# First loads in one queue, each asked for when a stage of the first tile has passed, and small constants 64 bytes wide

## The chip, the cores and the metric

The kernel runs on one core of a Trainium2 chip. The metric is the device time of one launch in microseconds (us), with all weights and inputs in the chip's memory (HBM) at the start. Everything is float32. One execution was recorded by the hardware profiler, and every duration below comes from that one.

## The reference

A sequence of 512 tokens, 1024 wide, passes two two-layer transformer blocks, one after the other. Each layer is a mixer (several kinds of attention) and a feed-forward part with a short convolution. Only the first steps of the first layer are touched directly:

```python
h = x                                                   # 512 x 1024
y = h * rsqrt(mean(h*h, -1) + EPS) * even_norm1[0]      # rmsnorm
qa, ka, va, qd, kd, vd = split_cols(y @ even_w_in[0], EVEN_IN_SPLIT)
o_a = moba_attention(...);  o_b = diff_attention(...)
h = h + concat(o_a, o_b) @ even_w_out[0]
h = h + conv_ffn(rmsnorm(h, ffn_norm[0]), ...)          # and so on, four layers
```

## The kernel before

**Products.** A float32 product is made of three single-pass products in the type fp32r. Each operand is split into a high part and the rest: activations into hh and hl (or pairs of k tiles), weights into wh and wl. Method mm3 issues the three: low times high (L356), high times low (L357), high times high (L358). In each, one 128-column operand is stationary (loaded into the array first), and the other is streamed past it, mostly 512 columns. In t_tile the weights are stationary ("b<-hh,wl": streamed hh, stationary wl); in r_tile the activations are stationary ("b<-wh,hh", "b<-wh,k", "b<-wh,e"). Transposes and the products of attention weights with values are plain float32 matmuls.

**Weights.** Class Stream loads the weights in the order of use as 455 blocks of at most 512 KB on SyncE's (SP) queue into three buffers wr (RAW = 3). prep makes wh on ScalarE (L299) and wl on VectorE (L300), four buffers each (HB = 4), and then issues the next loads.

**The start.** The tokens lie in four tiles x0 to x3 of 128 tokens. build issues x0, the gain row (512 KB, broadcast to all partitions, on ScalarE's queue), the identity matrix, x1, the first two weight blocks, x2 and x3, all at once. pre_norm returns three stages for a token tile: first, the sum of squares on ScalarE (L420); second, the scale factor on GpSimd (L403, L404) and the scaling on VectorE (L425); third, eight transposes on TensorE (L432) and the split into hh (ScalarE, L390) and hl (VectorE, L391). staged runs the stages of the four tiles as a pipeline, and fill(t) multiplies tile t with the first two weight blocks; vrest multiplies all four tiles with the next two, and so on. The Tile scheduler orders the instructions on each engine when the program is built; at run time each engine takes its own in that fixed order and waits for what it needs.

**Buffers.** All tiles lie in the on-chip memory at fixed places. They are placed one after another in the order of first use, each rounded up to a multiple of 32 bytes per partition. Blocks b8 hands out three tiles of 8192 bytes, named e; the first two are taken by the first pre_norm, the third later. Blocks blk hands out 42 tiles of 2048 bytes, named k. The constants on the way are cols_sb (584 columns, 2336 bytes), mhalf (64 bytes) and neglam (one column, 4 bytes).

Of the kernel before, what the change touches and what calls it, by code (L numbers as in the profile page):

```python
# [9 lines left out]
F32 = mybir.dt.float32  # L10
F32R = mybir.dt.float32r
AF = mybir.ActivationFunctionType
# [4 lines left out]
P, S, D, NT, KT = 128, 512, 1024, 4, 8  # L17
# [234 lines left out]
class Blocks:  # L252


    def __init__(self, pool, prefix, n, shape):
        self.pool, self.shape, self.free, self.tag, self.n = pool, shape, deque(f"{prefix}{i}" for i in range(n)), {}, 0
        self.prefix = prefix
# [15 lines left out]
class Stream:  # L273


    def __init__(self, k, w, plan):
        self.k, self.w, self.plan = k, w, plan
        self.loaded = self.prepped = self.lo = self.hi = 0
        self.raw, self.parts = {}, {}

    def load(self):
        i = self.loaded
        raw = self.k.sb.tile([P, CH], F32, name=f"wr{i}", tag="wr", bufs=RAW)
        n = self.plan[i][2]
        self.k.nc.sync.dma_start(raw[:, :n], self.w[i, :, :n])
        self.raw[i] = raw
        self.loaded += 1
# [36 lines left out]
class Kernel:  # L324
# [63 lines left out]
    def split(self, hi, lo, src):  # L388

        self.nc.scalar.copy(hi, src)  # L390
        self.nc.vector.tensor_sub(lo, src, hi.bitcast(F32))  # L391
# [16 lines left out]
    def pre_norm(self, gsrc, goff, queue=None):  # L408

        nc = self.nc  # L410
        e = self.b8.get()
        grow = e[:, :D]
        (queue or nc.sync).dma_start(grow, self.row(gsrc, goff, D))
        hb = self.b8.get()
        hs = [hb[:, :D], hb[:, D:]]
        ss = {}

        def sumsq(t):
            s = self.small()
            nc.scalar.activation(e[:, D:], self.x[t], AF.Square, accum_out=s)  # L420
            ss[t] = s

        def scale(t):
            r = self.rstd(ss.pop(t), 1.0 / D)
            nc.vector.scalar_tensor_tensor(hs[t % 2], self.x[t], r, grow, op0=ALU.mult, op1=ALU.mult)  # L425

        def turn(t):
            for half in range(2):
                b = self.bank(2 * t + half)
                for j in range(4):  # L430
                    c = (4 * half + j) * P
                    nc.tensor.transpose(b[:, j * P:(j + 1) * P], hs[t % 2][:, c:c + P], self.ident)  # L432
                src = b.rearrange("p (k q) -> p k q", k=4)
                dst = (slice(None), slice(4 * half, 4 * half + 4), slice(t * P, (t + 1) * P))
                self.split(self.hh[dst], self.hl[dst], src)

        def end():
            self.b8.put(e, hb)

        def first(t):  # L440
            sumsq(t)

        def second(t):
            scale(t)

        self.junk = e[:, D:]
        return [first, second, turn], end
# [147 lines left out]
class Job:  # L595
# [15 lines left out]
    def tail(self):  # L611
        return self._tail(self)
# [127 lines left out]
class Block1:  # L740
# [69 lines left out]
        return tail  # L810

    def start(self):
        self.first = self.k.pre_norm(self.k.a["even_norm1"], 0, self.k.nc.scalar)

    def even(self):
        k, nc, a = self.k, self.k.nc, self.k.a
        stages, end = self.first
        Va, Vd = {}, {}
        parts, vb = [], {}

        def fill(t):
            if not parts:
                parts.extend(k.ws.get(*[("e", "va", c) for c in range(2)]))
            vb[t] = k.bank(2 * t)
            for c in range(2):
                k.r_tile(vb[t], parts[c], t, (2 * c, 2 * c + 1), S, start=c == 0, stop=c == 3)

        k.staged(stages, fill)
        end()
        self.vrest("e", "va", 2, vb, Va)  # L830
        vb = {t: k.bank(2 * t + 1) for t in range(NT)}
        self.vrest("e", "vd", 0, vb, Vd)
        self.lam()
        self.tables()
        nc.sync.dma_start(k.cols, a["cols"])
        at, n = COLS[2, "bg"]
        nc.vector.tensor_scalar(k.cols[:, at:at + 2 * n], k.cols[:, at:at + 2 * n], 0.5, None, op0=ALU.mult)
        store, out, tabs = {}, {}, {}

        def begin(p):  # L840
            def f(job):
                if p < 4:
                    tabs[p] = [self.table(2 * p), self.table(2 * p + 1)]
                else:
                    tabs[p] = [self.table(4 + p)] * 2
            return f

        def free_qk(p, tail):
            def f(job):
                fns = tail(job)  # L850
                first = fns[0]

                def g():
                    k.blk.put(*store.pop(p))
                    k.blk.put(tabs[p][0])
                    if p < 4:
                        k.blk.put(tabs[p][1])
                    first()
                    if p == 3:
                        k.blk.put(*Va.values())  # L860
                return [g] + fns[1:]
            return f

        def tab(p):
            return lambda hd, t, n: tabs[p][hd][:, 384 - t * P:]

        jobs = []
        for p in range(4):
            jobs.append(Job(k, Job.PAIR, self.heads64(store, p), tab(p), out, lambda p=p: p in store, begin(p),
                            free_qk(p, self.pair_tail(Va, lambda hd, p=p: (2 * p + hd) * 64, store, p, tabs, out, p))))  # L870
        for h in range(4):
            p = 4 + h
            jobs.append(DiffJob(k, self.heads64(store, p), tab(p), out, lambda p=p: p in store, begin(p),
                                free_qk(p, self.diff_tail(Vd, h, out, p))))

        def dense():
            for p in range(8):
                while p - 2 in store:
                    yield NEED
                yield from self.qk_proj("e", p, store)  # L880
            while 3 not in out:
                yield NEED
            yield from self.out_half("e", out)

        k.weave(dense(), k.attention(jobs), 800)
        k.blk.put(*Vd.values())
        return self.out_rest("e", out, 0)
# [9 lines left out]
            V[t] = k.blk.get()  # L897
            k.evac(V[t], vb[t])

    def lam(self):  # L900
        k, nc, a = self.k, self.k.nc, self.k.a
        b = k.blk.get()
        nc.sync.dma_start(b[:, :256], k.row(a["diff_lambda"], 0, 256))
        v = b[:, :256].rearrange("p (a b d) -> p a b d", a=2, b=2)
        pr = b[:, 256:384].rearrange("p (a d) -> p a d", a=2)
        s, e = k.small(2), k.small(2)
        nc.vector.tensor_mul(pr, v[:, :, 0], v[:, :, 1])
        nc.vector.tensor_reduce(s, pr, axis=mybir.AxisListType.X, op=ALU.add)
        nc.scalar.activation(e, s, AF.Exp)
        nc.vector.tensor_sub(k.neglam, e[:, 1:2], e[:, 0:1])  # L910
        nc.vector.tensor_scalar_add(k.neglam, k.neglam, -0.2)
        nc.sync.dma_start(k.subln, k.row(a["diff_subln"], 0, P))
        nc.vector.tensor_scalar(k.subln, k.subln, 0.8, None, op0=ALU.mult)
        k.blk.put(b)
# [926 lines left out]
def build(tc, a, plan):  # L1841
    nc = tc.nc
    with ExitStack() as ctx:
        sb = ctx.enter_context(tc.tile_pool(name="sb", bufs=1))
        ps = ctx.enter_context(tc.tile_pool(name="ps", bufs=1, space=PSUM))
        dram = ctx.enter_context(tc.tile_pool(name="dram", bufs=1, space=DRAM))
        k = Kernel(tc, a, plan, sb, ps, dram)
        k.x = [k.const(f"x{t}", [P, D]) for t in range(NT)]
        xin = a["x"][0].rearrange("(t p) d -> t p d", p=P)
        k.ident = k.const("ident_sb", [P, P])  # L1850
        k.cols = k.const("cols_sb", [P, a["cols"].shape[1]])
        b1 = Block1(k)
        nc.sync.dma_start(k.x[0], xin[0])
        b1.start()
        nc.scalar.dma_start(k.ident, a["ident"])
        nc.sync.dma_start(k.x[1], xin[1])
        k.ws.load()
        k.ws.load()
        for t in range(2, NT):
            nc.sync.dma_start(k.x[t], xin[t])  # L1860
        k.mhalf = k.const("mhalf", [P, 16])
        nc.gpsimd.memset(k.mhalf, -0.5)
        k.neglam = k.const("neglam", [P, 1])
        k.subln = k.const("subln_sb", [P, P])
        k.hh = k.const("hh", [P, KT, S], F32R)
        k.hl = k.const("hl", [P, KT, S], F32R)
        ff = b1.even()
        ff = b1.odd(ff)
        b2 = Block2(k)
        ff = b2.mix(0, ff)  # L1870
        ff = b2.mix(1, ff)
        b2.end(ff)
# [39 lines left out]
```

## Time and profile before

| | us |
|---|---|
| median of three runs | 2867.37 (2866.7 to 2872.15) |
| the profiled execution | 2869.32 |
| its span on the core | 2867.5 |
| TensorE busy | 2822.6 |
| TensorE's first instruction | 14.63 |
| first matmul with weights | 19.35 |

The profile gives for each engine its busy time, for groups of instructions the line, the operation, out<-in by the program's names (buffer numbers left out) and the mean duration, and in the timeline each instruction with its start. Engines are PE (TensorE matmul), PEld (its loads of the stationary operand), DVE (VectorE), ACT (ScalarE), POOL (GpSimd) and SP (SyncE); a q behind the name is the engine's queue. TensorE's granted clock is 0.999 of full speed over the span. The duration of a matmul contains the pipeline's depth, so in a stream the distance from one start to the next is what each costs.

### The profile page before, as it was taken

Reading aid. Unit: us, or ns where it says so; the run is one execution under the profiler, and the core shown is the slowest. Engines: PE = TensorE matmul, PEld = TensorE weight load, DVE = VectorE, ACT = ScalarE, POOL = GpSimd, SP = SyncE. Lnnn points to the kernel's source line nnn. Section 1 sums busy time; section 2 is a strip of 40 time slices with the busy share of each in tenths; the row PEclk is TensorE's granted clock in tenths of the full one; section 3 lists DMA queues with packets and bytes.
Section 4 is the critical chain, followed back from the end, with each engine's and each line's share of the span. In section 5 each row is a group of like instructions: output and inputs, shape, how many; then the busy total and the mean of one; then the engine's idle time right before and its main releaser. Section 6 shows DMA issues by size and latency. Waiting matters only on the chain.

```text
span 2867.5 us, 34913 instructions
## 1 busy us (share of the span) xinstructions
PE 2822.6 (98%) x13612; PEld 2309.6 (81%) x13612; DVE 1538.3 (54%) x2687; ACT 1112.3 (39%) x1928; POOL 102.8 (4%) x192
## 2 busy tenths in 40 slices
PE   7999999999999999999999999999999999999999
PEld 6778888888788888787777888888887777888887
DVE  4566544244764443377655465552685544666633
ACT  3453433224533332245433344441454434344421
POOL 1000000000000000020000010000120000100000
PEclk9999999999999999999999999999999999999999
DMA  4542323334322233232234222333221332333232
GB/s 160 156 127 83 103 96 101 104 100 129 100 85 95 95 101 103 79 99 79 79 100 123 97 96 95 103 103 101 89 86 63 103 118 89 103 96 99 95 101 74
DMA packets 93651, 287.19 MB, mean 100 GB/s; under 512 B 12544, under 2 KB 15488, under 8 KB 93486
## 3 DMA queue, kind: packets, MB, share of 16 engines
q1 hardware_dynamic: 92526, 283.18, 31.6%
q8 instruction: 107, 1.75, 0.3%
q10 hardware_dynamic: 864, 1.64, 0.2%
q14 instruction: 58, 0.48, 0.1%
q0 software_dynamic: 96, 0.14, 0.0%
HBM read 258.38 MB, written 2.15 MB: 91 GB/s over the span
## 4 chain that ended last, share of the span: by engine, by line
PE 68%; issue 24%; DVE 4%; DMA 2%; POOL 1%; ACT 1%; SPq 0%; POOLq 0%; DVEq 0%; ACTq 0%
PE b L356 21%; PE b L358 21%; PE b L357 21%; PE b L1528 1%; PE b L655 1%; DMA k<-k 1%; PE b L362 1%; POOL s L404 1%; DMA wr<-in_w_dram 1%; DVE wl L300 1%; PE b L1783 1%; PE b L432 1%; PE b L1831 0%; DVE e L425 0%; PE b L1812 0%
## 5 line engine op out<-in xcount | busy, mean ns | idle before, releaser
L356 PE MATMUL b<-hh,wl 128*128 128x512 f32 (+1 forms) x2368 | 903.6, 382 | 1.6 <-ACT hh L390 1.0
L358 PE MATMUL b<-hh,wh 128*128 128x512 f32 (+1 forms) x2368 | 898.1, 379 | 0.0
L357 PE MATMUL b<-hl,wh 128*128 128x512 f32 (+1 forms) x2368 | 897.3, 379 | 0.0
L300 DVE TENSOR_TENSOR wl<-wr,wh 128x1024 fp32r<-128x1024 f32 (+1 forms) x421 | 511.5, 1217 | 538.8 <-ACT wh L299 536.8
L299 ACT CAST wh<-wr 128x1024 fp32r<-128x1024 f32 (+1 forms) x421 | 438.0, 1042 | 474.5 <-PE b L358 429.8
L356 PEld LDWEIGHTS b<-hh,wl 128*128 128x128 f32 x2368 | 445.1, 188 | 89.8 <-issue 7.9
L358 PEld LDWEIGHTS b<-hh,wh 128*128 128x128 f32 x2368 | 445.8, 188 | 83.4 <-issue 1.4
L357 PEld LDWEIGHTS b<-hl,wh 128*128 128x128 f32 x2368 | 446.2, 188 | 80.2 <-issue 2.0
L356 PE MATMUL b<-wh,k 128*128 128x512 f32 x900 | 352.9, 392 | 0.0
L357 PE MATMUL b<-wl,k 128*128 128x512 f32 x900 | 351.0, 390 | 0.0
L358 PE MATMUL b<-wh,k 128*128 128x512 f32 x900 | 350.6, 390 | 0.0
L356 PEld LDWEIGHTS b<-wh,k 128*128 128x128 f32 x900 | 169.1, 188 | 35.7 <-issue 0.8
L358 PEld LDWEIGHTS b<-wh,k 128*128 128x128 f32 x900 | 169.0, 188 | 35.4
L357 PEld LDWEIGHTS b<-wl,k 128*128 128x128 f32 x900 | 169.0, 188 | 33.9
L1231 ACT ACTIVATE e<-b,cols_sb 128x512 f32<-128x512 f32 x88 | 68.3, 776 | 153.7 <-PE b L358 153.7
L1232 DVE SCALAR_TENSOR_TENSOR e<-b,cols_sb,e 128x511 f32<-128x511 f32 x88 | 65.7, 746 | 104.6 <-ACT e L1231 104.4
L1221 DVE SCALAR_TENSOR_TENSOR e<-b,cols_sb,e 128x511 f32<-128x511 f32 x44 | 33.0, 749 | 159.2 <-ACT e L1220 159.2
L1220 ACT ACTIVATE e<-b,cols_sb 128x512 f32<-128x512 f32 x44 | 34.3, 778 | 178.1 <-PE b L358 178.1
L632 ACT ACTIVATE k<-k,s 128x256 f32<-128x256 f32 (+4 forms) x144 | 75.2, 523 | 59.5 <-DVE s L630 55.7
L357 PE MATMUL b<-wl,hh 128*128 128x512 f32 (+2 forms) x256 | 92.8, 362 | 0.4 <-DVE wl L300 0.4
L356 PE MATMUL b<-wh,hl 128*128 128x512 f32 (+2 forms) x256 | 93.1, 364 | 0.0
L358 PE MATMUL b<-wh,hh 128*128 128x512 f32 (+2 forms) x256 | 91.8, 360 | 0.0
(192 smaller groups left out, 3021.7 us busy)
## 6 DMA issues: line engine op xcount, KB each, us to landing
wr<-in_w_dram SPq DMA_DIRECT2D x451, 512.0 KB, 3.5
k<-k SPq DMA_DIRECT2D x186, 128.0 KB, 2.4
k<-brev SPq DMA_DIRECT2D x20, 256.0 KB, 4.0
x<-in_x_dram SPq DMA_DIRECT2D x4, 512.0 KB, 7.4
k<-in_rpb_dram SPq DMA_DIRECT2D x16, 128.0 KB, 3.2
wr<-in_w_dram SPq DMA_DIRECT2D x4, 448.0 KB, 3.2
e<-in_ffn_norm_dram SPq DMA_DIRECT2D x2, 512.0 KB, 3.7
e<-in_norm_mix_pre_dram SPq DMA_DIRECT2D x2, 512.0 KB, 4.5
```

The lines of the kernel that those rows point to most:

```text
L299: nc.scalar.copy(hi[:, :n], raw[:, :n])
L300: nc.vector.tensor_sub(lo[:, :n], raw[:, :n], hi[:, :n].bitcast(F32))
L356: mm(out, sl, mh, start=start, stop=False)
L357: mm(out, sh, ml, start=False, stop=False)
L358: mm(out, sh, mh, start=False, stop=stop)
L362: self.nc.tensor.matmul(out, s, m, start=i == 0, stop=i == len(pairs) - 1)
L404: nc.gpsimd.tensor_tensor(r, a, self.mhalf[:, :w], op=ALU.pow)
L632: nc.scalar.activation(s[:, c], s[:, c], AF.Exp, bias=mx[:, i:i + 1], scale=-1.0, accum_out=sm[:, i:i + 1])
L1220: nc.scalar.activation(c, b, AF.Identity, bias=self.col(("cb",), m), scale=self.col(("cw", 2), m))
L1221: nc.vector.scalar_tensor_tensor(c[:, 1:], b[:, :S - 1], self.col(("cw", 1), m), c[:, 1:], op0=ALU.mult, op1=ALU.add)
L1231: nc.scalar.activation(y, b, AF.Identity, bias=self.col(("cb",), mm), scale=self.col(("cw", 1), mm))
L1232: nc.vector.scalar_tensor_tensor(y[:, 1:], b[:, :S - 1], self.col(("cw", 0), mm), y[:, 1:], op0=ALU.mult, op1=ALU.add)
```

## The change

x0 and the gain row go first on SP's queue, in that order. The other first loads are held back: before each stands a one-column copy on GpSimd into the buffer that is to be loaded, which reads a column of a result that has to be there first. The two first weight blocks wait for x0's sum of squares (through a new constant, passed), x1 for x0's scaling, x2 for x0's second split, x3 for x1's first split, and the next weight blocks for x0's second split. The vectors for lam, subln and cols wait for the last tile's split. The identity goes first on ScalarE's queue, and a small Square on mhalf stands ahead of the first sum of squares. neglam grows from one column to 16, mhalf moves ahead of the e tiles, and passed (16 columns) is new.

```diff
 class Stream:
     def __init__(self, k, w, plan):
+        self.passed = None
     def load(self):
         raw = self.k.sb.tile([P, CH], F32, name=f"wr{i}", tag="wr", bufs=RAW)
+        if self.passed is not None:
+            self.k.nc.gpsimd.tensor_copy(raw[:, :1], self.passed)
         self.k.nc.sync.dma_start(raw[:, :n], self.w[i, :, :n])
...
-        hs = [hb[:, :D], hb[:, D:]]
+        hs = self.normed = [hb[:, :D], hb[:, D:]]
...
     def start(self):
-        self.first = self.k.pre_norm(self.k.a["even_norm1"], 0, self.k.nc.scalar)
+        self.first = self.k.pre_norm(self.k.a["even_norm1"], 0)
...
-        stages, end = self.first
+        (first, second, turn), end = self.first
+        passed = k.const("passed", [P, 16])[:, :1]
+        def ask(t, stage):
+            nc.gpsimd.tensor_copy(k.x[t][:, :1], stage)
+            nc.sync.dma_start(k.x[t], xin[t])
...
-        k.staged(stages, fill)
+        def sumsq(t):
+            first(t)
+            if t == 0:
+                nc.gpsimd.tensor_copy(passed, k.junk[:, :1])
+                k.ws.passed = passed
+                k.ws.load()
+                k.ws.load()
+        def scale(t):
+            second(t)
+            if t == 0:
+                ask(1, k.normed[0][:, :1])
+        def split(j, t):
+            return k.hl[:, j, t * P:t * P + 1].bitcast(F32)
+        def last(t):
+            turn(t)
+            if t < 2:
+                ask(2 + t, split(4 - 4 * t, t))
+            k.ws.passed = split(4, 0) if t == 0 else None
+            fill(t)
+        k.staged([sumsq, scale, last])
...
-        self.lam()
+        self.lam(split(4, NT - 1))
         self.tables()
+        nc.gpsimd.tensor_copy(k.cols[:, :1], split(4, NT - 1))
         nc.sync.dma_start(k.cols, a["cols"])
...
+        k.mhalf = k.const("mhalf", [P, 16])
+        nc.gpsimd.memset(k.mhalf, -0.5)
+        nc.scalar.dma_start(k.ident, a["ident"])
+        nc.scalar.activation(k.small(16), k.mhalf, AF.Square)
         nc.sync.dma_start(k.x[0], xin[0])
         b1.start()
-        nc.scalar.dma_start(k.ident, a["ident"])
-        nc.sync.dma_start(k.x[1], xin[1])
-        k.ws.load()
-        k.ws.load()
-        for t in range(2, NT):
-            nc.sync.dma_start(k.x[t], xin[t])
-        k.mhalf = k.const("mhalf", [P, 16])
-        nc.gpsimd.memset(k.mhalf, -0.5)
-        k.neglam = k.const("neglam", [P, 1])
+        k.neglam = k.const("neglam", [P, 16])[:, :1]
```

The order on the engines moves at the start alone. VectorE up to the first tiles' splits, before (numbers tell instances apart; wr_75 and wr_77 are the first two weight blocks, x_63 to x_66 the token tiles):

```order
L300 TENSOR_TENSOR wl_139<-wr_75,wh_138 128x1024
L300 TENSOR_TENSOR wl_147<-wr_77,wh_146 128x1024
L425 SCALAR_TENSOR_TENSOR e_72<-x_63,s_90,e_70 128x1024
L425 SCALAR_TENSOR_TENSOR e_72<-x_64,s_111,e_70 128x1024
L425 SCALAR_TENSOR_TENSOR e_72<-x_65,s_132,e_70 128x1024
L391 TENSOR_TENSOR hl<-b_5_96,hh 128x4x128
L391 TENSOR_TENSOR hl<-b_6_103,hh 128x4x128
```

and now (line numbers are four higher):

```order
L429 SCALAR_TENSOR_TENSOR e_77<-x_63,s_93,e_75 128x1024
L395 TENSOR_TENSOR hl<-b_6_101,hh 128x4x128
L304 TENSOR_TENSOR wl_118<-wr_86,wh_117 128x1024
L395 TENSOR_TENSOR hl<-b_7_108,hh 128x4x128
L304 TENSOR_TENSOR wl_128<-wr_89,wh_127 128x1024
L429 SCALAR_TENSOR_TENSOR e_77<-x_64,s_162,e_75 128x1024
L429 SCALAR_TENSOR_TENSOR e_77<-x_65,s_198,e_75 128x1024
L395 TENSOR_TENSOR hl<-b_12_168,hh 128x4x128
```

The first tile's scaling and splits now stand ahead of, and between, the two weight blocks.

GpSimd after its three table loads, before:

```order
L403 TENSOR_SCALAR s_89<-s_87 128x1
L404 TENSOR_TENSOR s_90<-s_89,mhalf 128x1
L403 TENSOR_SCALAR s_110<-s_94 128x1
L404 TENSOR_TENSOR s_111<-s_110,mhalf 128x1
L403 TENSOR_SCALAR s_131<-s_115 128x1
L404 TENSOR_TENSOR s_132<-s_131,mhalf 128x1
```

and now:

```order
L407 TENSOR_SCALAR s_92<-s_83 128x1
L288 COPY wr_86<-passed 128x1
L288 COPY wr_89<-passed 128x1
L408 TENSOR_TENSOR s_93<-s_92,mhalf 128x1
L828 COPY x_64<-e_77 128x1
L828 COPY x_65<-hl 128x1
L288 COPY wr_121<-hl 128x1
L288 COPY wr_124<-hl 128x1
L288 COPY wr_131<-hl 128x1
L407 TENSOR_SCALAR s_161<-s_99 128x1
L408 TENSOR_TENSOR s_162<-s_161,mhalf 128x1
```

The copies that hold loads back stand between the scale factors; the second tile's factor (s_162) stands behind five of them.

The places of the buffers move for the whole program. Start in each partition in bytes, by the two built programs, with the remainder to 64 in brackets:

| tile | before | after |
|---|---|---|
| first and second e | 35744, 43936 (32) | 38368, 46560 (32) |
| three wr, from | 52128 (32) | 88160 (32) |
| hh, hl | 65024, 81408 (0) | 55328, 71712 (32) |
| four wh, from | 100352 (0) | 100448 (32) |
| four wl, from | 116736 (0) | 116832 (32) |
| 42 k, from | 133120 (0) | 133216 (32) |
| third e | 151552 (0) | 151648 (32) |

Before, cols_sb (2336 bytes) leaves the remainder 32, and neglam, rounded from 4 to 32 bytes, takes it away again for all that lies behind. After, mhalf, neglam and passed take 64 bytes each.

## Rows read from the trace of the kernel before

**Rows 1.** The page, busy time, share of the span and instructions of each engine.
```profile
PE 2822.6 (98%) x13612; PEld 2309.6 (81%) x13612; DVE 1538.3 (54%) x2687; ACT 1112.3 (39%) x1928; POOL 102.8 (4%) x192
```
**Rows 2.** Timelines of the start: start us, us, engine line op out<-in [idle before].
```profile
6.05 1.06 ACT L420 ACTIVATE e<-x 128x1024 f32<-128x1024 f32 x1 [3.10 <-DMA x<-in_x_dram]
7.29 0.18 POOL L403 TENSOR_SCALAR s<-s 128x1 f32<-128x1 f32 x1 [4.23 <-ACT e L420]
7.56 0.57 POOL L404 TENSOR_TENSOR s<-s,mhalf 128x1 f32<-128x1 f32 x1
...
10.88 2.50 DVE L300 TENSOR_TENSOR wl<-wr,wh 128x1024 fp32r<-128x1024 f32 x2 [10.88 <-ACT wh L299]
...
13.29 1.28 DVE L425 SCALAR_TENSOR_TENSOR e<-x,s,e 128x1024 f32<-128x1024 f32 x1
...
14.63 5.07 PE L432 MATMUL b<-ident_sb,e 128*128 128x128 f32 x21 [14.63 <-DVE e L425]
...
19.35 0.78 PE L356 MATMUL b<-wh,hl 128*128 128x512 f32 x1
...
43.18 0.59 ACT L398 COPY k<-b 128x512 f32<-128x512 f32 x1 [2.13 <-PE b L358]
```
**Rows 3.** The page, DMA issues: out<-in, xcount, size each, median us to landing.
```profile
wr<-in_w_dram SPq DMA_DIRECT2D x451, 512.0 KB, 3.5
...
x<-in_x_dram SPq DMA_DIRECT2D x4, 512.0 KB, 7.4
```
**Rows 4.** Matmuls by line, tiles and shape: count | busy us, mean ns.
```profile
L356 PE MATMUL b<-hh,wl 128*128 128x512 f32 x2112 | 832.4, 394 | 0.6 <-DVE k L1606 0.6
...
L356 PE MATMUL b<-wh,k 128*128 128x512 f32 x900 | 352.9, 392 | 0.0
...
L356 PE MATMUL b<-k,wl 128*128 128x512 f32 x220 | 87.9, 399 | 1.2 <-DVE k L1606 0.7 <-DVE k L391 0.5
...
L356 PE MATMUL b<-hh,wl 128*128 128x256 f32 x256 | 71.2, 286 | 1.0 <-ACT hh L390 1.0
L356 PE MATMUL b<-wh,hl 128*128 128x512 f32 x160 | 63.2, 396 | 0.0
...
L356 PE MATMUL b<-wh,hl 128*128 128x256 f32 x64 | 18.1, 283 | 0.0
```
**Rows 5.** Tile e, 610 to 650 us (first layer): duration ns min/median/max.
```profile
L432 PE MATMUL b<-ident_sb,e x32: 270/272/329, 623.6 to 643.7; 128*128 128x128 f32 x32
L356 PE MATMUL b<-wh,e x16: 394/394/400, 613.8 to 634.4; 128*128 128x512 f32 x16
L357 PE MATMUL b<-wl,e x16: 392/399/399, 614.1 to 634.6; 128*128 128x512 f32 x16
L358 PE MATMUL b<-wh,e x16: 390/392/394, 614.3 to 634.9; 128*128 128x512 f32 x16
```
**Rows 6.** The same, 1195 to 1235 us (second layer).
```profile
L356 PE MATMUL b<-wh,e x16: 389/389/395, 1196.8 to 1219.5; 128*128 128x512 f32 x16
L357 PE MATMUL b<-wl,e x16: 389/389/393, 1197.0 to 1219.8; 128*128 128x512 f32 x16
L358 PE MATMUL b<-wh,e x16: 389/389/389, 1197.2 to 1220.0; 128*128 128x512 f32 x16
```
**Rows 7.** Timeline of PE, first and last of twelve in a row, first layer.
```profile
619.39 0.39 PE L356 MATMUL b<-wh,e 128*128 128x512 f32 x1
...
621.96 0.39 PE L358 MATMUL b<-wh,e 128*128 128x512 f32 x1
```
**Rows 8.** The same, second layer.
```profile
1202.22 0.39 PE L356 MATMUL b<-wh,e 128*128 128x512 f32 x1
...
1204.71 0.39 PE L358 MATMUL b<-wh,e 128*128 128x512 f32 x1
```
**Rows 9.** The same, 838 to 872 us (transposes between the first two layers).
```profile
L432 PE MATMUL b<-ident_sb,e x32: 270/272/276, 841.6 to 866.1; 128*128 128x128 f32 x32
```
**Rows 10.** Tile e streamed in plain float32 (L1528), the whole span.
```profile
L1528 PE MATMUL b<-e,k x128: 592/592/645, 1339.8 to 2260.4; 128*64 128x512 f32 x128
```

More of the change, by code (lines that the diff above doesn't have):

```diff
@@ L812, in start @@
     def start(self):
-        self.first = self.k.pre_norm(self.k.a["even_norm1"], 0, self.k.nc.scalar)
+        self.first = self.k.pre_norm(self.k.a["even_norm1"], 0)
     def even(self):
         k, nc, a = self.k, self.k.nc, self.k.a
-        stages, end = self.first
+        (first, second, turn), end = self.first
         Va, Vd = {}, {}
         parts, vb = [], {}
+        xin = a["x"][0].rearrange("(t p) d -> t p d", p=P)
+        passed = k.const("passed", [P, 16])[:, :1]
+        def ask(t, stage):
+            nc.gpsimd.tensor_copy(k.x[t][:, :1], stage)
+            nc.sync.dma_start(k.x[t], xin[t])
         def fill(t):
@@ L898, in vrest, with lam @@
             k.evac(V[t], vb[t])
-    def lam(self):
+    def lam(self, passed):
         k, nc, a = self.k, self.k.nc, self.k.a
         b = k.blk.get()
+        nc.gpsimd.tensor_copy(b[:, :1], passed)
+        nc.gpsimd.tensor_copy(k.subln[:, :1], passed)
         nc.sync.dma_start(b[:, :256], k.row(a["diff_lambda"], 0, 256))
```

## The prediction

> **What bounds the kernel now.** I read the busy times first. TensorE is busy for 2822.6 of 2867.5 us, 98%; VectorE has 54% and ScalarE 39% [rows 1]. So two things can move the time: the 45 us in which TensorE is idle, and the duration of its matmuls. Of the idle time 14.6 us lie at the start in one piece [rows 2], and 30 us are spread over the rest. The change means to move the first piece. But it also moves every buffer, so after the timeline of the start I looked at matmuls whose operands lie at different places.
>
> At the start, x0's sum of squares begins at 6.05 us and its scale factor is ready at 8.13 (7.56 + 0.57), yet the scaling comes at 13.29, since VectorE's order has both weight blocks first (10.88 and 2.50 long). So transposes start at 14.63 and weight matmuls at 19.35, and from there TensorE runs on: the first bank of the first product is copied out until 43.18 [rows 2], and its 96 matmuls of 0.226 [rows 8] and the late transposes fill that stretch. What the change can win is that this end at 43.2 comes sooner.
>
> **The start, step by step.** A 512 KB block lands a median of 3.5 us after its issue in the stream, and the four x tiles, all asked at once, took 7.4 [rows 3]. Now x0 goes nearly alone: I take 4.5 us as its landing (ends: 3.5 after the issue, or 6.05 as now). Sum of squares 1.25, then GpSimd: its order is the copy into passed, the first half of the factor, two copies into wr, the second half. Copies aren't in the trace; the small operation at 7.29 has 0.18 and the next starts 0.27 later [rows 2], so four steps of 0.27 and 0.57 end at about 7.4. VectorE scales until 8.7 (1.28), eight transposes, about a microsecond (21 took 5.07 with their waits [rows 2]), end at 9.7. The weights, asked at 6.5, land at 10.0 and 11.2; their splits (1.06 on ScalarE, as an operation of that width took, 1.25 on VectorE [rows 2]), mixed with x0's splits, let the first matmuls start at 12.5 instead of 19.35.
>
> That is 7 us sooner, but it isn't kept. After x0's 12 matmuls TensorE waits for x1, whose load was asked at 9.0, and now the tiles follow each other by landings: copy 0.3, landing 3.5, sum 1.25, factor 0.85, scaling 1.28, transposes 1, split 1.3 make 9.5 us for one tile. x2 is asked when x0's second split is done (13.2), x3 when x1's first split is done, and VectorE's order puts x2's scaling ahead of that split, so x3 is asked at about 21.3 and lands at 25. Its split ends at 30.4. Of the 96 matmuls 52 are then left, 11.8 us, which end at 42.5. The gain at 43.2 is 0.7 us. Ends: with 2.5 us for a landing and no stall the work itself, 25 us from 12.5, ends at 37.4, 6 us won; with the slow rows (7.4 for a landing once, copies that wait behind a VectorE operation of 1.28) 4 us are lost. Queued behind the waiting copies on GpSimd are the factors of x1 to x3, which the order shows, and they are in this walk. The vectors for lam and cols are asked some 15 us later than now and used from the first attention on; their cover is the 96 matmuls of the next product, 22 us. The extra Square on ScalarE runs before x0 has landed. Both at nothing.
>
> **The places of the buffers.** Before, hh, hl, wh, wl, the k tiles and the third e start at a multiple of 64 bytes; the first two e and wr lie 32 bytes off. After, all of them lie 32 off: 2336 bytes of cols_sb leave 32, and neglam, 32 bytes before, no longer takes it away. Whether that costs can be read from the trace of before, since an e tile is now and then the stationary operand of a single-pass matmul. In the first layer that tile is one that lies 32 off: medians of 394, 399 and 392 ns for the three lines [rows 5]. In the second layer the same lines, the same shapes, work on the third e, which starts at a multiple of 64: 389, 389 and 389 [rows 6]. Mean difference 6.0 ns. Starts say the same: twelve in a row take 2.57 us for 11 distances in the first layer [rows 7], 233.6 ns each, and 2.49 in the second [rows 8], 226.4; difference 7.3, with 0.01 us of rounding at each end. I take 6.7. The streamed operand is a wh or wl, at 0 in both, so it is the stationary one that pays.
>
> Plain float32 shows nothing of it: transposes of an e that lies 32 off have a median of 272 ns [rows 5], of the third e 272 too [rows 9]. And streamed e tiles of both kinds take 592 ns at the minimum and the median alike [rows 10]. So only single-pass matmuls pay, by their stationary operand.
>
> After the change nearly all of them do. In [rows 4] stand the groups of L356, and L357 and L358 have as many: (2112 + 900 + 220 + 256 + 160 + 64) x 3 = 11,136 matmuls, and their stationary operands are wl, wh, hl, hh and k, all moved from 0 to 32. At 6.7 ns that is 74.6 us (66.8 at 6.0, 81.3 at 7.3). TensorE is busy without a gap through them, so it lies on the path. I take 3 us off for the 30 us of spread idle time, where a wait may shrink because TensorE comes later; the attention's score matmuls, which I haven't counted, may add as much. For VectorE and ScalarE no row here splits by place; they have 46% and 61% of idle time as cover [rows 1]. DMAs into wr land 32 off already.
>
> The streamed operand moves too. No row shows a streamed fp32r operand that lies 32 off; the nearest is plain float32, with no cost [rows 10], and from above I bound it by what the stationary one pays, another 75 us. I take 0, as the row says.
>
> **Sum.** -0.7 + 74.6 - 3 = +71 us. Against the profiled execution (2869.32, 2867.5 of span) that is 2940; the median of the runs is 2 us lower, so 2938. Own range of this case: 6.0 ns and the best start give +58, 7.3 ns, no absorption and the worst start +88, so 2925 to 2955.
>
> **Rivals.**
> First, not slower: the place as such costs nothing. Then the difference in [rows 5, 6] comes from the two operands lying differently (32 against 0), and as both move by 32 it is gone. Its price is 0 instead of 74.6, and it decides as soon as the matmuls keep their distance of 226 ns. Time: the start alone, 2867.4 - 0.7 = 2867, with the start's ends 2861 to 2871. For it: I have seen no pair with both operands at 32. Against it: the slower pace stays through twelve matmuls [rows 7], whichever of wh and wl is streamed.
> The Trainium skill, page "SBUF — State Buffer", section "Specifications (TRN2)", gives lines of 16 bytes for the memory. A tile that lies 32 off starts on such a line as well as one at 64; by that rule the new places cost nothing, the same 2867. The trace doesn't agree: 394, 399 and 392 ns against 389 [rows 5, 6].
>
> Second: the streamed operand pays as well, another 74.6 us: 2938 + 75 = 3013. For it: the streamed 2048 bytes come from the same memory, and fp32r streams in one pass, 226 ns from start to start, where plain float32 takes longer and may hide it. Against it: [rows 10].
>
> Third, that the change does what it says and wins: x0's 7 us are kept. It needs landings of 2.5 us for x1 to x3, and gives 6 us at the most, less than a tenth of what the places cost; it is in the ranges above.
>
> **Chances.** Stationary operand pays: 0.70. Both pay: 0.10. Neither pays: 0.20. A measurement of this kernel can tell about 0.2%, 5.7 us, from no change. The first two are slower. Of the third, 0.14 lies within 0.2%, 0.05 is faster by more, 0.01 slower. So slower 0.81, same 0.14, faster 0.05. The range takes in the first and the third case, 2860 to 2960, and leaves out the second and the tails.
>
> **What would show it.** In the profile after: the groups of L360 to L362 with a mean 6 to 7 ns above [rows 4] and the medians of the second layer's e matmuls at 394, 399, 392 as in [rows 5]; TensorE's busy time near 2897. If they stay at 389, the first rival holds; at 13 ns more, the second. At the start: the first weight matmul near 12.5, a pause of some 5 us before x1's, the end of the first product at 42 to 43. I am wrong if the matmuls keep their pace, or if the start alone moves the end by more than 6 us.

## The result, and the profile after

The changed kernel takes 2901.55 us, the median of four runs (2899.24 to 2903.69), against 2867.86 for the kernel before on the same chip. The ratio is 1.0117, with a 95% interval from 1.0105 to 1.0129: slower by about 33.7 us. The forecast was 2938, with a range of 2925 to 2955 for its main case. The sign is right, and the place too (TensorE's matmuls take longer), but the size is a little under half of the 71 us that were said.

The page of the kernel after, busy time, share of the span (2901.9 us) and instructions, which answers to [rows 1]:

```profile
PE 2856.9 (98%) x13612; PEld 2307.0 (79%) x13612; DVE 1538.9 (53%) x2687; ACT 1113.8 (38%) x1929; POOL 105.1 (4%) x206
```

TensorE is busy 34.3 us longer with the same 13,612 matmuls, and idle for 45.0 us as before (44.9). The span grew by 34.4. So the whole difference is longer matmuls, and no new wait. Which ones, the groups of TensorE tell, by line, tiles and shape (xcount | busy us, mean ns | idle before), which answer to [rows 4]:

```profile
L360 PE MATMUL b<-hh,wl 128*128 128x512 f32 x2112 | 843.8, 400 | 0.6 <-DVE k L1642 0.6
L362 PE MATMUL b<-hh,wh 128*128 128x512 f32 x2112 | 837.9, 397 | 0.0
L361 PE MATMUL b<-hl,wh 128*128 128x512 f32 x2112 | 836.9, 396 | 0.0
L360 PE MATMUL b<-wh,k 128*128 128x512 f32 x900 | 352.7, 392 | 0.0
...
L360 PE MATMUL b<-k,wl 128*128 128x512 f32 x220 | 87.8, 399 | 1.2 <-DVE k L1642 0.7 <-DVE k L395 0.5
...
L360 PE MATMUL b<-hh,wl 128*128 128x256 f32 x256 | 70.2, 282 | 1.0 <-ACT hh L394 1.0
L360 PE MATMUL b<-wh,hl 128*128 128x512 f32 x160 | 64.3, 403 | 0.8 <-ACT wh L303 0.8
```

Two groups of the kernel before that were not shown yet, for the other two lines of mm3:

```profile
L358 PE MATMUL b<-hh,wh 128*128 128x512 f32 x2112 | 826.2, 391 | 0.0
L357 PE MATMUL b<-hl,wh 128*128 128x512 f32 x2112 | 824.9, 391 | 0.0
```

Three things are to be seen. The groups that stream hh or hl past wh or wl with 512 columns grew by 11.4, 11.7 and 12.0 us: 35.1 us, which is the whole result. The groups with k as an operand, 3360 matmuls on three lines, did not move: 352.9 to 352.7, 87.9 to 87.8, although k moved by as many bytes as wh. And the same hh with 256 columns became faster, 71.2 to 70.2 on this line. A cost that every moved stationary operand pays would have raised all three.

The start, from the timeline of all engines (start us, us, engine line op out<-in, idle before), which answers to [rows 2]:

```profile
4.99 1.06 ACT L424 ACTIVATE e<-x 128x1024 f32<-128x1024 f32 x1 [2.29 <-DMA x<-in_x_dram]
...
7.59 1.28 DVE L429 SCALAR_TENSOR_TENSOR e<-x,s,e 128x1024 f32<-128x1024 f32 x1 [7.59 <-POOL s L408]
8.93 1.57 PEld L436 LDWEIGHTS b<-ident_sb,e 128*128 128x128 f32 x8 [8.93 <-DVE e L429]
8.93 1.97 PE L436 MATMUL b<-ident_sb,e 128*128 128x128 f32 x8 [8.93 <-DVE e L429]
8.94 0.18 POOL L828 COPY x<-e 128x1 f32<-128x1 f32 x1 [1.38 <-DVE e L429]
...
11.69 0.79 PE L360 MATMUL b<-wh,hl 128*128 128x512 f32 x1 [0.79 <-ACT wh L303]
...
13.56 1.11 POOL L828 COPY x<-hl 128x1 f32<-128x1 f32 x1 [4.43 <-DVE hl L395]
13.71 1.06 ACT L424 ACTIVATE e<-x 128x1024 f32<-128x1024 f32 x1 [0.64 <-DMA x<-in_x_dram]
13.97 0.63 PE L360 MATMUL b<-wh,hl 128*128 128x512 f32 x1
...
14.40 0.63 PE L361 MATMUL b<-wl,hh 128*128 128x512 f32 x1
...
15.98 1.28 DVE L429 SCALAR_TENSOR_TENSOR e<-x,s,e 128x1024 f32<-128x1024 f32 x1 [1.35 <-POOL s L408]
...
16.85 0.40 PE L361 MATMUL b<-wl,hh 128*128 128x512 f32 x1
16.85 0.19 PEld L362 LDWEIGHTS b<-wh,hh 128*128 128x128 f32 x1
17.08 0.40 PE L362 MATMUL b<-wh,hh 128*128 128x512 f32 x1
17.32 0.86 PEld L436 LDWEIGHTS b<-ident_sb,e 128*128 128x128 f32 x8 [0.28 <-DVE e L429]
...
21.79 0.87 PE L436 MATMUL b<-ident_sb,e 128*128 128x128 f32 x6 [3.37 <-DVE e L429]
...
23.53 0.33 SPq L829 DMA_DIRECT2D x<-in_x_dram  x1
```

and the last copy of the first product, on ScalarE (its start stands for the end of that product, here and in the runs below):

```profile
44.92 0.59 ACT L402 COPY k<-b 128x512 f32<-128x512 f32 x1 [2.16 <-PE b L362]
```

x0's scaling comes at 7.59 instead of 13.29, and the first weight matmul at 11.69 instead of 19.35, more than 7 us sooner. But TensorE then waits for tiles (3.37 us ahead of x2's transposes alone), the last tile is asked for only at 23.53, and the first product ends at 44.92, 1.7 us later than the 43.18 of [rows 2].

### The profile page after: what moved, and what is told of

Its sections match the earlier page's. It is cut to its first block, busy times and chain, and to the rows that moved or that the text cites. A ratio compares the mean times of both kernels' runs of the same rounds, so it can differ in the third digit from the quotient of the medians.

```text
span 2901.9 us, 34939 instructions
## 1 busy us (share of the span) xinstructions
PE 2856.9 (98%) x13612; PEld 2307.0 (79%) x13612; DVE 1538.9 (53%) x2687; ACT 1113.8 (38%) x1929; POOL 105.1 (4%) x206
## 3 DMA queue, kind: packets, MB, share of 16 engines
q10 hardware_dynamic: 720, 1.11, 0.1%
## 4 chain that ended last, share of the span: by engine, by line
PE 68%; issue 25%; DVE 3%; DMA 2%; POOL 1%; ACT 1%; SPq 0%; POOLq 0%; DVEq 0%; ACTq 0%
PE b L360 21%; PE b L362 21%; PE b L361 21%; PE b L659 1%; PE b L1564 1%; DMA k<-k 1%; POOL s L408 1%; PE b L366 1%; PE b L1819 1%; PE b L1867 0%; PE b L1849 0%; DVE wl L304 0%; PE b L1848 0%; DVE e L429 0%; DMA x<-in_x_dram 0%
## 5 line engine op out<-in xcount | busy, mean ns | idle before, releaser
L360 PE MATMUL b<-hh,wl 128*128 128x512 f32 (+1 forms) x2368 | 914.0, 387 | 1.6 <-ACT hh L394 1.0
L362 PE MATMUL b<-hh,wh 128*128 128x512 f32 (+1 forms) x2368 | 908.6, 384 | 0.0
L361 PE MATMUL b<-hl,wh 128*128 128x512 f32 (+1 forms) x2368 | 908.0, 384 | 0.0
L360 PE MATMUL b<-wh,k 128*128 128x512 f32 x900 | 352.7, 392 | 0.0
L1256 ACT ACTIVATE e<-b,cols_sb 128x512 f32<-128x512 f32 x44 | 34.3, 779 | 184.3 <-PE b L362 184.3
L400 DVE COPY e<-b 128x512 f32<-128x512 f32 (+1 forms) x112 | 63.1, 564 | 55.7 <-PE b L1867 24.8
```

The lines of the kernel that those rows point to most:

```text
L360: mm(out, sl, mh, start=start, stop=False)
L361: mm(out, sh, ml, start=False, stop=False)
L362: mm(out, sh, mh, start=False, stop=stop)
L400: self.nc.vector.tensor_copy(out, src)
L1256: nc.scalar.activation(c, b, AF.Identity, bias=self.col(("cb",), m), scale=self.col(("cw", 2), m))
```

## The experiments

**The question.** Two theories fit what the kernel before showed in [rows 5, 6]. Theory A, the prediction's: a single-pass matmul pays when its stationary operand starts 32 bytes off a multiple of 64, wherever the streamed one lies. Theory B: it pays when its two operands start at different places modulo some power of two, wherever they lie. The table of places in the section on the change gives remainders to 64, by which hh and wh look alike after the change. To 256 they don't:

| tile | before, mod 256 | after, mod 256 |
|---|---|---|
| first and second e | 160 | 224 |
| hh, hl | 0 | 32 |
| wh, wl, k, third e | 0 | 96 |

So by theory B hh and hl have gone apart from wh and wl by 64, k has stayed with wh and wl, and the e tiles were the pair that lay apart before. The kernels below move single buffers, by constants that nobody reads, and leave all work as it is unless it is said.

**b_pad64: the kernel before, with the weights and k moved by 64 bytes.** All stationary operands stay at multiples of 64; hh and hl part from wh and wl by 64.

```diff
         k.hl = k.const("hl", [P, KT, S], F32R)
+        pad = k.const("padw", [P, 16])
+        k.nc.gpsimd.memset(pad, 0.0)
```

> The kernel before, its order untouched, with a 64-byte constant placed between hl and wh: hh and hl keep the remainder 0 to 256 bytes, and wh, wl, the k tiles and the third e move to the remainder 64. All starts that were multiples of 64 still are. Own place (the theory of the prediction: a stationary operand that lies 32 bytes off a multiple of 64 pays): no change, 2867 us, the groups of hh with wl and wh stay at 379 to 394 ns. Distance (what counts is the distance between the starts of the stationary and the streamed operand, modulo 256): the 6336 matmuls of 512 columns with hh streamed past wh or wl go from 227 to 233 ns from start to start, as in the changed kernel, +35 us, 2902 us; the groups wh with k keep 390 to 392.

Measured: 2896.82 us, ratio 1.0098 (1.0082 to 1.0115). TensorE's groups:

```profile
L356 PE MATMUL b<-hh,wl 128*128 128x512 f32 x2112 | 843.0, 399 | 0.6 <-DVE k L1606 0.6
L358 PE MATMUL b<-hh,wh 128*128 128x512 f32 x2112 | 837.1, 396 | 0.0
L357 PE MATMUL b<-hl,wh 128*128 128x512 f32 x2112 | 835.9, 396 | 0.0
L356 PE MATMUL b<-wh,k 128*128 128x512 f32 x900 | 352.7, 392 | 0.0
...
L356 PE MATMUL b<-hh,wl 128*128 128x256 f32 x256 | 70.0, 281 | 1.0 <-ACT hh L390 1.0
```

The same three groups grow as after the change (10.6, 10.9 and 11.0 us), k stays, and 256 columns gain. Nothing of the start was touched and no operand left its multiple of 64. Theory A falls: it gives no change here. A 64-byte constant in the wrong place costs this kernel 28.6 us.

**a_near: the change, with passed placed ahead of hh.** In the order of the places passed then stands before the big tiles, so hh, hl, wh, wl, k and the third e all start at 96 modulo 256. All of them still lie 32 off a multiple of 64.

```diff
+        k.passed = k.const("passed", [P, 16])[:, :1]
         k.subln = k.const("subln_sb", [P, P])
...
-        passed = k.const("passed", [P, 16])[:, :1]
+        passed = k.passed
```

> The changed kernel with passed placed ahead of subln instead of behind hl, so that hh, hl, wr, wh, wl, k and the third e all have the remainder 96 to 256; order and waits stay. Own place: all still lie 32 off a multiple of 64, no change against the changed kernel, 2901 us. Distance: all of hh, wh, wl and k lie alike, the 6336 matmuls go back to 227 ns, -35 us; what stays is the start, 1 to 2 us later than in the kernel before: 2868 to 2870 us.

Measured: 2869.67 us, ratio 1.0006 (0.9996 to 1.0015).

```profile
L360 PE MATMUL b<-hh,wl 128*128 128x512 f32 x2112 | 832.0, 394 | 0.6 <-DVE k L1642 0.6
L362 PE MATMUL b<-hh,wh 128*128 128x512 f32 x2112 | 826.0, 391 | 0.0
L361 PE MATMUL b<-hl,wh 128*128 128x512 f32 x2112 | 824.3, 390 | 0.0
```

The means are those of the kernel before, with every operand 32 off. This is the counterpart of b_pad64: the own place costs nothing, the distance alone does. And it gives the price of the rest of the change, the reordered start: +1.5 us by the medians, with an interval from about -1 to +4. Its first product ends at 44.68 us, as late as after the change.

**b_pad32_96: three places.** The kernel before with wh and wl at 32 and k at 128, while hh stays at 0. Both kinds of pair lie apart now, though k is at a multiple of 64.

```diff
         k.hl = k.const("hl", [P, KT, S], F32R)
+        pad = k.const("padw", [P, 8])
+        k.nc.gpsimd.memset(pad, 0.0)
...
         end()
+        pad = k.const("padk", [P, 24])
+        k.nc.gpsimd.memset(pad, 0.0)
         self.vrest("e", "va", 2, vb, Va)
```

> The kernel before with 32 bytes between hl and wh and 96 between wl and k: remainders hh 0, wh and wl 32, k 128. Own place: every matmul with wh or wl stationary pays 6.7 ns (some 7800), +50 us; those with k stationary (2700) keep 390 to 392 ns, since 128 is a multiple of 64. Distance: both kinds pay, by how much at 32 (hh streamed, w stationary) and at 96 (w streamed, k stationary) is not known; at 6 ns each +35 and +16 us.

Measured once: 2925.47 us, 57.3 above the kernel before on that chip (2868.2).

```profile
L356 PE MATMUL b<-hh,wl 128*128 128x512 f32 x2112 | 843.9, 400 | 0.6 <-DVE k L1608 0.6
...
L356 PE MATMUL b<-wh,k 128*128 128x512 f32 x900 | 358.6, 399 | 0.0
L357 PE MATMUL b<-wl,k 128*128 128x512 f32 x900 | 356.9, 397 | 0.0
```

Here the k groups pay as well, 5.7 to 5.9 us a line. Distances of 32 (hh) and 96 (k) cost about as much as 64.

**b_off16: hh and hl at 16, k at 128.** This asks whether a smaller distance is cheaper. hh and hl are cut out of tiles 256 bytes longer, from the byte 16 on.

```diff
-        k.hh = k.const("hh", [P, KT, S], F32R)
+        k.hh = k.const("hh", [P, KT * S + 64], F32R)[:, 4:4 + KT * S].rearrange("p (k s) -> p k s", k=KT)
```

(hl likewise, and a constant of 32 columns ahead of k, where b_pad32_96 has 24.)

> The kernel before with hh and hl starting 16 bytes into their place and 128 bytes between wl and k: remainders hh and hl 16, wh and wl 0, k 128. Own place: the 480 matmuls with hh or hl stationary may pay, all others not, +3 us. Distance: at -16 (hh streamed) and at 128 (w streamed, k stationary) a cost of its own; at 128 the e matmuls of the changed kernel had 232 ns, so the 2700 with k stationary cost +14 us; -16 is not known.

Measured once: 2906.74 us, +38.5.

```profile
L356 PE MATMUL b<-hh,wl 128*128 128x512 f32 x2112 | 840.9, 398 | 0.6 <-DVE k L1608 0.6
...
L356 PE MATMUL b<-wh,k 128*128 128x512 f32 x900 | 357.3, 397 | 0.0
```

16 bytes apart still costs, a little less; 128 apart costs too, so 128 doesn't count as 0.

**b_pad256 and b_off4: the two ends.** b_pad256 is b_pad64 with 64 columns instead of 16 (the weights and k move by 256 bytes). b_off4 is b_off16 with `1:1 + KT * S` and without the constant ahead of k: hh and hl start at 4 bytes, the smallest step there is.

```diff
+        pad = k.const("padw", [P, 64])
...
-        k.hh = k.const("hh", [P, KT, S], F32R)
+        k.hh = k.const("hh", [P, KT * S + 64], F32R)[:, 1:1 + KT * S].rearrange("p (k s) -> p k s", k=KT)
```

> The kernel before with 256 bytes between hl and wh: hh and hl at 0, wh, wl and k at 256 to 512. If the distance counts modulo 256, no change: 2868 us, the groups of hh with wl and wh at 389 at the median. If it counts modulo 512, 256 is a distance of its own, and they may pay 5 to 7 ns: 2895 to 2905 us.

> The kernel before with hh and hl starting 4 bytes into their place; all else keeps its remainder. If any distance but 0 costs, the groups of hh with wl and wh pay 4 to 7 ns, 2893 to 2910 us. If the distance counts in lines of 16 bytes, 4 bytes leave the streamed start in its line but move it inside; then the cost is smaller than at 16 bytes (2907 us) or nil, 2868.

Measured, once each: b_pad256 2868.15 us (kernel before on that chip: 2868.59), b_off4 2930.99, +62.4, more than was expected of it. First b_pad256:

```profile
L356 PE MATMUL b<-hh,wl 128*128 128x512 f32 x2112 | 832.5, 394 | 0.6 <-DVE k L1606 0.6
```

and b_off4:

```profile
L356 PE MATMUL b<-hh,wl 128*128 128x512 f32 x2112 | 853.7, 404 | 0.6 <-DVE k L1606 0.6
...
L356 PE MATMUL b<-wh,k 128*128 128x512 f32 x900 | 352.7, 392 | 0.0
...
L356 PE MATMUL b<-hh,wl 128*128 128x256 f32 x256 | 72.2, 290 | 1.0 <-ACT hh L390 1.0
```

A distance of 256 counts as none, and 128 doesn't, so of the powers of two it is 256 by which the places have to agree. Four bytes cost the most of all, 21.3 us in this group against 11.4 after the change, and there 256 columns lose as well.

**All distances together.** For each single-pass matmul of 512 columns I took the distance from its start to the next start in the trace, and the two operands' places from the built program. Means in ns, with intervals of 300 and more left out; the distance is the start of the stationary operand minus that of the streamed one, modulo 256 (where a row has two distances, the values stand in their order):

| distance | mean, ns | seen in |
|---|---|---|
| 0 | 227.0 to 227.8; with k streamed 227.9 to 229.0 | before, after (wh, wl and k), b_pad64 (wh, wl and k), b_pad256 |
| 252 | 237.0 to 238.6 | b_off4, hh and hl streamed |
| 4 | 232.2 to 232.6 | b_off4, hh and hl stationary |
| 16, 240 | 229.6 to 230.5, 231.6 to 231.7 | b_off16 |
| 32, 224 | 233.1 to 233.3, 233.3 to 233.7 | b_pad32_96 |
| 64, 192 | 233.3 to 233.4, 227.8 to 230.1 | after, b_pad64 |
| 96 | 234.1 to 234.3 | b_pad32_96 (wh, wl with k) |
| 128 | 232.7 to 232.9 | b_off16 (wh, wl with k) |
| 160 | 231.9 and 235.8 | before (wh and wl with the first two e) |

At distance 0 it is 227 whether both lie at 0 (before), both at 64 (wh with k in b_pad64) or both at 96 (after). The rows of the table come from different loops, so a difference of 1 or 2 ns between two of them isn't to be put down to the distance. Nor is the distance the whole account of the size: at 160 the matmuls of one loop that stream wh and those that stream wl are 3.9 ns apart, and at 192 one group has 227.8, no more than at 0.

**v_all_x: the two lessons used.** a_near, with the first two e tiles brought to 96 as well, and with x1, x2 and x3 all asked for when x0 is scaled, in place of one after the other.

```diff
+        pe = k.const("pade", [P, 32])
+        nc.gpsimd.memset(pe, 0.0)
         nc.scalar.dma_start(k.ident, a["ident"])
...
+        pe = k.const("pads", [P, 96])
+        nc.gpsimd.memset(pe, 0.0)
+        k.passed = k.const("passed", [P, 16])[:, :1]
...
-                ask(1, k.normed[0][:, :1])
+                for u in range(1, NT):
+                    ask(u, k.normed[0][:, :1])
...
-            if t < 2:
-                ask(2 + t, split(4 - 4 * t, t))
```

> The changed kernel with all tiles at the remainder 96 to 256 (the two first e too), and with x1, x2 and x3 all asked as soon as x0 is scaled, instead of each after a stage of the tile before. Theory of the start: in the changed kernel the first product ends 1.7 us later than before because x3 is asked only at 23.5 us; with it asked at 9.2 it lands some 10 us sooner, and the first product ends at 41 to 42 us instead of 44.9 (43.2 in the kernel before). With the first two e at distance 0 some 144 matmuls lose 6 ns, -0.9 us. Time 2864 to 2866. Rival: the weight blocks set the end, and it stays at 44 to 45 us; time 2868 to 2869.

Measured: 2865.99 us, ratio 0.9993 (0.9984 to 1.0002). Tile e from 600 to 650 us in the first layer, duration ns min/median/max:

```profile
L360 PE MATMUL b<-wh,e x16: 389/389/390, 611.0 to 631.2; 128*128 128x512 f32 x16
L361 PE MATMUL b<-wl,e x16: 389/389/390, 611.2 to 631.4; 128*128 128x512 f32 x16
L362 PE MATMUL b<-wh,e x16: 389/389/390, 611.5 to 631.6; 128*128 128x512 f32 x16
```

and on ScalarE the end of the first product:

```profile
41.18 0.59 ACT L402 COPY k<-b 128x512 f32<-128x512 f32 x1 [2.13 <-PE b L362]
```

The medians 394, 399, 392 of [rows 5], from which the prediction was made, are now 389 throughout, with e at 96 and not at a multiple of 64: the last word on theory A, from the very rows that it came from. The first product ends at 41.18, 2.0 us sooner than in [rows 2] and 3.7 sooner than after the change. The time is 2.6 us below the kernel before, and the interval still holds 1.

**v_warm: the slow first matmuls.** After the change the first weight matmuls start 0.43 us apart (13.97, 14.40) and later 0.23 (16.85, 17.08). v_warm is v_all_x with 24 products of the identity with itself ahead of the transposes (the trace has two matmuls for each) and 10 of hh with itself ahead of the first weight matmul; nobody reads them.

```diff
         b1.start()
+        wb = k.bank(7)
+        for _ in range(24):
+            nc.tensor.matmul(wb[:, :P], k.ident, k.ident, start=True, stop=True)
...
+            if t == 0:
+                wb = k.bank(7)
+                for _ in range(10):
+                    nc.tensor.matmul(wb[:, :P], k.hh[:, 0, :P], k.hh[:, 0, :P], start=True, stop=True)
             fill(t)
```

> The same with 24 matmuls of the identity with itself ahead of the first transposes and 10 of hh with itself ahead of the first weight matmul, whose results nobody reads. In the changed kernel the first weight matmuls start 0.43 us after each other for 3 us, later 0.23. If what TensorE did before sets this, the first 12 now take 0.23 each and 2 us are won where TensorE then has no wait: the first product ends up to 2 us sooner than in v_all_x, 2862 to 2865 us. If the first product's end is set by the loads, nothing is won.

Measured: 2866.14 us, ratio 0.999 (0.9981 to 0.9998). Timeline of TensorE and of its loads:

```profile
5.10 7.06 PE L1903 MATMUL b<-ident_sb 128*128 128x128 f32 x48 [5.10 <-DMA ident_sb<-in_ident_dram]
12.00 1.04 PE L436 MATMUL b<-ident_sb,e 128*128 128x128 f32 x8
...
16.06 0.39 PE L360 MATMUL b<-wh,hl 128*128 128x512 f32 x1
16.29 0.40 PE L361 MATMUL b<-wl,hh 128*128 128x512 f32 x1
...
21.73 1.54 PEld L436 LDWEIGHTS b<-ident_sb,e 128*128 128x128 f32 x8 [1.15 <-DVE e L429]
```

and the stretch from 22 to 25 us (busy time and count of each engine, then the granted clock, DMA share and GB/s):

```profile
22.00:25.00 3.00, 2.94 (x15) 2.54 (x13) 2.60 (x3) 2.58 (x5) 0.36 (x1) 0.50 0.22 89
```

The first weight matmuls do start 0.23 us apart, but the identity lands only at 5.10, so the added products hold TensorE until 12.0 and put off x0's transposes from 8.86 (v_all_x) to 12.00. A second loss follows: TensorE waits 1.08 and 0.91 us for x1's and x2's scaling, and from 21.8 to 25.2 us its granted clock reads 0.50, the lower of its two levels (1.2 GHz). The first product ends at 44.68, 3.5 us later than in v_all_x, so nothing is won there. That the runs are still level with v_all_x shows that a few microseconds at the start don't all reach the end. By the starts of the same weight blocks' splits on ScalarE, v_warm's trace is 3.5 us behind up to 80 us, 1.6 at 340 and level at 1040; what takes the lead away, no run here shows. Both versions beat the changed kernel by 1.2%. v_warm's interval lies just below 1 and v_all_x's holds it, and neither differs from the kernel before by the 0.2% that can be told.

## Why the prediction was half right

**The step that failed: "The places of the buffers".** It read [rows 5] against [rows 6] as a cost of the stationary operand's own place. In those rows two things differ: e lies at 160 in one and at 0 in the other, and with that its distance to wh, which lies at 0 in both. The prediction saw this as its first rival, and then got the rival's condition wrong: "as both move by 32 it is gone". hh went from 65024 to 55328, by -9696, and wh from 100352 to 100448, by +96; only their remainders to 64 both changed by 32. Distances between the operands of each pair, from the same table, would have shown 64 for hh with wh and 0 for k with wh. What the runs showed in its place: a single-pass matmul of 512 columns is slowed when its two operands start at different places modulo 256 bytes, and their own places don't count (b_pad64 +28.6 us with hh, hl, wh, wl and k at multiples of 64, a_near +1.5 with all of them 32 off).

That the sign came out right is luck. The prediction's argument gives the same +71 us for a_near, which differs from the changed kernel in where passed stands and in nothing else, and a_near is level with the kernel before. It is passed, 64 bytes wide and placed between hl and wh, that makes the change slow.

**What that does to the term of +74.6.** It was 11,136 matmuls at 6.7 ns. The 3360 with k paid nothing: -22.5. The 960 with 256 columns were to pay 6.4 and got faster, 3.3 on the three lines with hh streamed: -9.7. The remaining 6336 + 480 matmuls were given 45.7 and took 38.0 (35.1, and 2.9 for the three r_tile groups with hh, some of it in the start): -7.7, since a distance of 64 costs 5.5 ns a matmul by busy time and not 6.7. Together 34.7, against 34.3 by the busy times of the pages. So the count failed most, the price per matmul little.

**The streamed operand** was taken at 0 with an upper bound of another 75. As a second, separate payer it doesn't exist: a_near moves it and nothing is paid.

**The absorption of 3 us** didn't come: TensorE's idle time is 44.9 before and 45.0 after.

**The start.** The mechanism was right: some 7 us won at the first matmul, and lost again because the tiles follow one another by landings. Scaling was forecast at 7.4 (7.59), the first matmul at 12.5 (11.69 and 12.95 for the first two lines). The size was off, and that lies with GpSimd, whose slow copies the prediction had in its worse end alone: the copy at 13.56 took 1.11 us where the one at 8.94 took 0.18. VectorE's split of a weight block runs beside it from 13.42 for 1.21 us, and both end within 0.05 us of each other. The same happens at 22.40, and x3 is asked for at 23.53 instead of 21.3. The two copies, 0.9 us longer each, make most of these 2.2 us. The end was forecast at 42.5 (30.4 and 11.8, its own terms, make 42.2) and came at 44.92, so the term is +1.7 and not -0.7, inside its ends of -6 and +4.

**The slow first matmuls** were missed as well. From 13.54 to 16.53 us seven distances between starts are 0.43 us each, nearly twice the later 0.23: 1.4 us. The granted clock reads 1.00 there, but the pace speaks against it. Eight loads for the transposes took 1.57 us at 8.93 and 0.86 at 17.32, and v_warm has 1.54 for eight where its granted clock reads 0.50, the lower level. By this pace TensorE, idle until 8.93, ran at 1.2 GHz until some 16.5 us, though no row names that clock. The Trainium skill, page "TensorE: Matmul & The Clock Gate", section "Wait — 56ns, not 53.3ns?", gives start distances of 426.7 ns for 512 columns at 1.2 GHz. The seven distances agree, 2.99 us in all. In the kernel before, 21 transposes came right ahead of the first weight matmul and took up most of the slow stretch (eight loads at 14.63 took 1.57 us there too); now there are eight, with pauses of 0.79 and 0.47. The 1.4 us cost the end nothing, for x1's transposes at 17.32 wait for x1's scaling, which is done at 17.26 (15.98 + 1.28).

**The range.** The terms that it lists for the upper end of +88 make 85 (81.3 + 4), unless the 3 us of the score matmuls are in it.

**The start's price.** By a_near's runs the start as a whole costs 1.5 us, and zero is in that interval.

**The second rival** (both operands pay, 3013) is excluded by a_near. **The third** (the start wins up to 6) is not seen: v_all_x, which asks for all tiles early, ends the first product 2 us sooner and no more.

**What stays open.** Why the distance costs anything, why 4 bytes cost more than 16 or 64, and why 256 columns gain at most distances, no run here shows. Nor do the runs tell which stationary operand counts. While one matmul streams, the next one's stationary operand is already being loaded (from 16.85 us for the matmul that starts at 17.08), and in each loop here it mostly comes from the same kind of buffer as the matmul's own.

## What to carry to other kernels

Before trusting a change that adds or widens a small buffer, work out where every large buffer starts now, and compare the two operands of each frequent matmul with each other, modulo 256 bytes, not each with a round number. One pair of rows that differ in place supports every theory in which anything about the place counts: name what else differs between them before multiplying it by 11,136. Where work is queued behind waits on a slow side engine, price its instructions beside what runs on VectorE at that moment, not alone.

## What was not expected of the hardware

- Single-pass fp32r matmuls of 512 columns start 227 to 229 ns apart when stationary and streamed operand start at the same place modulo 256 bytes. Otherwise it is 228 to 239, and 233 for the groups that the change slowed. In this kernel that is 28.6 us (1.0%) for a 64-byte constant and 62.4 us (2.2%) for four bytes.
- The Trainium skill, page "TensorE: Matmul & The Clock Gate", section "Step-by-step: what each phase is for", says that TensorE has two independent read ports, so that loading the next stationary operand doesn't steal read bandwidth from the running matmul. What is measured here differs in so far as the pace depends on where the two operands lie against each other; whether it is their reading that collides, no run shows.
- With 256 columns it is the other way round for most distances: 120 ns at distance 0, 115 to 118 at 64 and 192, 123 to 125 at 252 (hh and hl streamed past wh; hh past wl contains waits).
- One-column copies on GpSimd took 0.18 us, or 1.11 beside a VectorE operation with two inputs in the on-chip memory.
- The granted clock read 1.00 over TensorE's first stretch of work, where its loads had the pace that they have at 0.50 in v_warm. Distances between starts tell more there.
